# Where the squares of a norm run, in which order a list scheduler puts them, and when the next FFN may begin: one change to a two-layer trunk on eight cores

## The chip, the cores and the metric

The kernel runs on the eight cores of one Trainium2 chip. Each core holds 1280 of the 10240 tokens and does the whole computation for them. The metric is the device time of the slowest core in microseconds (us). Executions come in a fast and a slow state: in the slow one a die's cores show a lower granted clock.

Words used below: in this kernel TensorE (PE) does the matmuls, ScalarE (ACT) activations, VectorE (DVE) and GpSimd (POOL) elementwise work. FFN(l,s) is FFN s (0 or 1) of layer l. Its *first matmuls* make gate and up (22 pieces), its *second matmuls* bring the product back to 1024 channels. "Norm 6" is the RMSNorm in front of FFN(1,1), "norm 5" the one in front of layer 1's pooling, "norm 3" the one in front of FFN(0,1). *h* is a norm's shifted output (`sb_hbuf`), which the matmuls behind it read. A *bank* is one of the result buffers of TensorE (`ps`): the program writes it again only when ScalarE or VectorE has read it (in before, on core 6, TensorE stood 7.46 us until ScalarE had taken the first Silus, `sb_sg`, from theirs). A *gap* is time in which TensorE stands still.

## The reference, cut to what matters

```python
def run_trunk(x, ...):                       # x: (tokens, 1024)
    for l in range(2):
        mod = silu(cvec) @ ada_w[l] + ada_b[l]            # shifts, scales, gates
        x = x + 0.5 * g1 * swiglu(modulate(x, ...), ...)  # FFN(l,0)
        h = modulate(x, norm_g[l, 1], sh2, sc2)
        out = conv_attn_mixer(h, ...) if l == 0 else pool_mixer(h, ...)
        x = x + g2 * out
        x = x + 0.5 * g3 * swiglu(modulate(x, ...), ...)  # FFN(l,1)
    return rms_norm(x, final_g)
# modulate(x) = x * rsqrt(mean(x*x) + eps) * g * (1 + scale) + shift
# swiglu(h)   = (silu(h @ w1_gate) * (h @ w1_up)) @ w2, inner width 2816
# pool_mixer  = per channel group: (window mean - token) @ pool_w, window 2, 4, 8, 16
```

Seven norms, four FFNs, one attention and convolution mixer, one pooling mixer. The pooling of a token needs its neighbours up to 8 places away, so a tile's pooling needs the neighbouring tile's projected values.

## The kernel before

Activations stand transposed (channels on partitions, 8 chunks of 128) in three tiles of 512, 512 and 256 tokens. The program is written as small threads that yield operations; a list scheduler in Python commits one at a time and so fixes the instruction order on each engine before anything runs. The engines then go through their lists in order, waiting on semaphores: on core 6 of before ScalarE waits eight times, 0.55 to 0.64 us each, for VectorE's scalings between 1261 and 1274 us, and takes the first Silus of FFN(1,1), which stand behind in its list, only at 1276.41, though their matmuls run from 1254.42. What the scheduler thinks of time decides only the order:

```python
    def est(self, o):                        # class Sched
        t = self.free[o.eng]
        for d in self.deps_of(o):
            t = max(t, d.t_end)              # (cut)
        if o.tab is not None and o.tab != self.tab:
            t += 1280.0                      # ScalarE would have to load a table
        return t
    # run(): of all threads' next operations, on all engines, take the one with the
    # smallest (est, prio, seq).  Ln and Exp share a table, Silu has another.
```

The trace of before shows the tables on core 4: a load of 1.28 us ends just before tile 0's Ln at 43.37 us, Exp follows at 44.06 without one, and the next load, at 79.37, stands in front of the first Silus. The 18 loads take 1283 ns on average.

A norm: squares of 8 chunks by a plan, sums into `acc`, ones-matmuls over partitions on TensorE, Ln and Exp on ScalarE, then 8 scalings on VectorE (`sb_nt`) and 8 shifts on ScalarE (`sb_hbuf`, which the matmuls read).

```python
    def main(self):
        P8 = [(POOL, False)] * 6 + [(ACT, True)] * 2    # (engine of the square, summed by TensorE?)
        MX = [(ACT, False), (POOL, False), (ACT, False), (ACT, False),
              (POOL, False), (ACT, False), (ACT, True), (DVE, True)]
        ...
        yield from self.ffn(0, 1)
        self.prefetch(AF.Silu)
        S.spawn(self.mixer1(), 3)
        for t in range(3):
            S.spawn(self.norm(t, 5, 1, 1, P8), 0)
        yield from self.ffn(1, 0)
        for t in range(3):
            S.spawn(self.norm(t, 6, 1, 2, MX), 0)        # norm 6 enters the queues here
        yield self.wait("mix1done")                      # all 24 pooling residuals
        self.prefetch(AF.Silu)
        ...
        yield from self.ffn(1, 1)

    # mixer1, layer 1's pooling
        for t in range(3):
            yield self.wait(("h", t, 1, 1), 8)
            for i in range(4 * t, min(4 * t + 4, 10)):
                yield from ztile(i, t)                   # projection of tile t
            if t >= 1:
                ...
                yield from pout(t - 1)                   # pooling of the tile before
        yield from pout(2)
```

Weights stream through a ring of 512 KB slots (`sb_ring`); 72 of the slots are the modulation weights (`adaw`), strewn among the others.

The softmax here doesn't subtract the row's maximum and nothing guards it: scores larger than these inputs give would overflow.

Of the kernel before, what the change touches and what calls it, by code (L numbers as in the profile page):

```python
# [9 lines left out]
AF = mybir.ActivationFunctionType  # L10
# [35 lines left out]

class Op:
    __slots__ = ("eng", "fn", "reads", "writes", "cost", "is_dma", "nbytes", "key", "deps", "marked", "sig", "dval",
                 "t_end", "tab")

    def __init__(self, eng, fn, reads, writes, cost, is_dma=False, nbytes=0, key=None):
        self.eng, self.fn, self.reads, self.writes, self.cost = eng, fn, reads, writes, cost
        self.is_dma, self.nbytes, self.key = is_dma, nbytes, key
        self.deps = ()
        self.marked = False
        self.tab = None
        self.sig = 0
        self.dval = 0
        self.t_end = 0.0
# [17 lines left out]
class Sched:  # L77
# [56 lines left out]
    def est(self, o):  # L134
        t = self.free[o.eng]
        for d in self.deps_of(o):
            td = d.t_end
            if td > t:
                t = td
        if o.tab is not None and o.tab != self.tab:  # L140
            t += 1280.0
        return t

    def commit(self, o):
# [32 lines left out]
    def run(self):  # L177
        while self.threads:
            best, bk = None, None
            changed = False  # L180
            for t in sorted(self.threads, key=lambda t: (t.prio, t.seq)):
                while isinstance(t.head, Wait) and t.head.pred():
                    self.advance(t)
                    changed = True
                h = t.head
                if h is None or isinstance(h, Wait):
                    continue
                k = (self.est(h), t.prio, t.seq)
                if bk is None or k < bk:
                    best, bk = t, k  # L190
            if best is None:
                if changed:
                    continue
                raise RuntimeError("deadlock: %s" % [(t.prio, t.gen.__name__) for t in self.threads])
            self.commit(best.head)
            self.advance(best)
# [79 lines left out]
class Builder:  # L276
# [392 lines left out]
        d = self.dummy  # L669
        self.S.post([self.act(d[0:1, 0:1], d[0:1, 1:2], func, [self.b_dummy], [self.b_dummy])], 0)  # L670

    def rstd(self, t, ver, plan):

        c0, n, v = TILES[t]
        acc = None
        if not all(pe for e, pe in plan):
            acc = yield from self.take(self.accp)
        done, got = ("sumd", t, ver), {}

        def squares():  # L680
            first = True
            for d in range(8):
                e, pe = plan[d]
                yield self.wait(("x", t, d), ver)
                x, bxx = self.xres[:, d, c0:c0 + n], self.bx[t][d]
                if first and not pe:
                    first = False
                    yield self.square(e, acc[1][:, 0:n], x, bxx, acc[0])
                    self.sigl(done)
                    continue  # L690
                sq = yield from self.take(self.sqp)

                def one(e=e, pe=pe, x=x, bxx=bxx, sq=sq, d=d):
                    s = sq[1][:, 0:n]
                    yield self.square(e, s, x, bxx, sq[0])
                    if pe:
                        got[d] = sq
                    else:
                        a = acc[1][:, 0:n]
                        yield self.tt(a, a, s, ALU.add, [acc[0], sq[0]], [acc[0]], POOL if e == POOL else DVE)  # L700
                        self.sqp.give(sq)
                        self.sigl(done)
                self.S.spawn(one(), 1)
        self.S.spawn(squares(), 0)
        parts = ([] if acc is None else [None]) + [d for d in range(8) if plan[d][1]]
        nacc = sum(1 for e, pe in plan if not pe)
        k = None
        for q, d in enumerate(parts):
            if d is None:
                yield self.wait(done, nacc)  # L710
                src = acc
            else:
                yield Wait(lambda d=d: d in got)
                src = got[d]
            if k is None:
                k = yield from self.bank()
            yield self.mm([(self.psv(k, n), self.onesf[:], src[1][:, 0:n], q == 0, q == len(parts) - 1)],
                          [src[0], self.b_onesf], [self.psb[k]], f32=True)
            (self.accp if d is None else self.sqp).give(src)
        ps, pb = self.psv(k, n), self.psb[k]  # L720
        rs = yield from self.take(self.rsp)
        br, r = rs[0], rs[1][:, 0:n]
        yield self.act(r, ps, AF.Ln, [pb], [br], bias=EPS, scale=1.0 / D)
        self.unbank(k)
        yield self.act(r, r, AF.Exp, [br], [br], scale=-0.5)
        return rs

    def square(self, e, out, x, bx, bo):
# [1 line left out]
            return self.act(out, x, AF.Square, [bx], [bo])  # L730
        return self.tt(out, x, x, ALU.mult, [bx], [bo], e)

    def norm(self, t, ver, l, i, engs, hfree=None, sh=ACT):
        c0, n, v = TILES[t]
        rs = yield from self.rstd(t, ver, engs)
        br, r = rs[0], rs[1][:, 0:n]
        if hfree is not None:
            yield Wait(hfree)
        asc, msb = self.asc[l], self.modsb[l]
        for c in range(8):  # L740
            yield self.wait(("mod", l, i, c // 2), 2)
            bm = self.b_mod[l][3 * i][c // 2]
            nt = yield from self.take(self.ntp)
            bn, nv = nt[0], nt[1][:, 0:n]
            yield self.stt(nv, self.xres[:, c, c0:c0 + n], asc[:, i, c, v:v + 1], r, ALU.mult, ALU.mult,
                           [self.bx[t][c], br, self.b_asc[l][i][c // 2]], [bn])

            def fin(c=c, nt=nt, bn=bn, nv=nv, bm=bm):
                hv, b = self.hbuf[:, c, c0:c0 + n], msb[:, 24 * i + c, v:v + 1]
                if sh == ACT:  # L750
                    yield self.act(hv, nv, AF.Identity, [bn, bm], [self.bh[t][c]], bias=b, scale=1.0)
                else:
                    yield self.ts(hv, nv, b, None, ALU.add, None, [bn, bm], [self.bh[t][c]])
                self.ntp.give(nt)
                self.sigl(("h", t, l, i))
            self.S.spawn(fin(), 0)
        self.rsp.give(rs)


# [1 line left out]
    def ffn(self, l, s):  # L761
        S = self.S
# [4 lines left out]
        def room(t, j):  # L767
            lo = self.aoff(t) + j * TILES[t][1]
            if (l, s) == (0, 1):
                if not self.has("attndone"):  # L770
                    return False
                if not self.has("outmm", 3) and (t == 2 or (t == 0 and lo + 512 > self.q_lo)):
                    return False
            if (l, s) == (1, 1) and not self.has("mix1done"):
                return False
            if j not in NJT[t]:
                NJT[t][j] = self.abuf("a%d_%d" % (t, j), lo, lo + TILES[t][1])
# [111 lines left out]

    def main(self):  # L890
        S = self.S
        P8 = [(POOL, False)] * 6 + [(ACT, True)] * 2
        MX = [(ACT, False), (POOL, False), (ACT, False), (ACT, False), (POOL, False), (ACT, False), (ACT, True), (DVE, True)]
        IN = [(ACT, True), (DVE, True)] * 4
        for t in range(3):
            S.spawn(self.norm(t, 1, 0, 0, IN), 0)
        S.spawn(self.mixer0(), 3)
        for t in range(3):
            S.spawn(self.norm(t, 2, 0, 1, P8, sh=DVE if t == 2 else ACT), 0)
        yield from self.ffn(0, 0)  # L900
        for t in range(3):
            S.spawn(self.norm(t, 3, 0, 2, MX, hfree=lambda: self.has("convdone")), 0)
        for t in range(3):
            S.spawn(self.norm(t, 4, 1, 0, P8), 0)
        yield from self.ffn(0, 1)
        self.prefetch(AF.Silu)
        S.spawn(self.mixer1(), 3)
        for t in range(3):
            S.spawn(self.norm(t, 5, 1, 1, P8), 0)
        yield from self.ffn(1, 0)  # L910
        for t in range(3):
            S.spawn(self.norm(t, 6, 1, 2, MX), 0)
        yield self.wait("mix1done")
        self.prefetch(AF.Silu)
        for t in range(3):
            S.spawn(self.final(t, 7, P8), 0)
        yield from self.ffn(1, 1)


# [455 lines left out]
    def mixer1(self):  # L1375
        S = self.S
# [82 lines left out]
                    self.sigl("pout")  # L1459
                S.spawn(fin(), 1)  # L1460

        for t in range(3):
            yield self.wait(("h", t, 1, 1), 8)
            for i in range(4 * t, min(4 * t + 4, 10)):
                yield from ztile(i, t)
            if t >= 1:
                for i in range(0, 4 * t + (4 if t == 1 else 2)):
                    yield self.wait(("z", i), 2)
                yield from pout(t - 1)
        yield from pout(2)  # L1470
        self.wfree(("poolw",))
        yield self.wait("pout", 24)
        self.sigl("mix1done")

    def final(self, t, ver, engs):
        c0, n, v = TILES[t]
        rs = yield from self.rstd(t, ver, engs)
        br, r = rs[0], rs[1][:, 0:n]
# [153 lines left out]
```

## Time and profile before

| | before |
|---|---|
| time, fast runs | 1569.4 us median of 4 (1568.4 to 1570.6) |
| TensorE busy on the slowest core | 1464.3 of 1568.1 us |
| ScalarE, VectorE, GpSimd busy | 448.7, 500.1, 305.5 us |
| table loads on ScalarE | 18 |

The chain that ended last is 84% TensorE: whatever keeps TensorE from working costs time, and hardly anything else does. The prediction shows where it stands. The following view adds what the stretch of layer 1's pooling looks like in 20 us windows (busy us of each engine with the number of instructions, then granted clock, DMA share, GB/s; core 6):

```profile
core 6: us, PE busy (x) PEld busy (x) DVE busy (x) ACT busy (x) POOL busy (x), PEclk, DMA share, GB/s
1200.00:1220.00 20.00, 13.30 (x123) 11.28 (x121) 10.40 (x14) 3.42 (x7) 11.86 (x19) 0.92 0.35 53
1220.00:1240.00 20.00, 12.30 (x90) 8.41 (x90) 14.82 (x23) 11.01 (x20) 5.17 (x5) 0.74 1.03 161
1240.00:1260.00 20.00, 11.87 (x36) 5.37 (x37) 12.67 (x22) 9.96 (x16) 4.86 (x7) 0.66 0.56 103
1260.00:1280.00 20.00, 12.54 (x52) 5.26 (x51) 11.67 (x20) 13.61 (x25) 0.00 (x0) 0.87 0.00 0
```

For 80 us TensorE works 12 to 13 us in 20, at a clock down to 0.66, and no other compute engine is near full; the DMA queue is, in one of the four windows. That is a stage of waits, not of work.

I split the span at marks that are easy to find in TensorE's timeline of each core: the first of an FFN's second matmuls (they read `sb_areg` and `sb_ring`) and the first projection of the pooling. All stage times below are medians over eight cores.

### The profile page before, as it was taken

How to read it: one execution, taken by the hardware profiler on the slowest of the kernel's cores; microseconds unless marked ns; L12 is line 12 of the kernel's file. 1: busy time of each engine (PE TensorE's matmuls, PEld its weight loads, DVE VectorE, ACT ScalarE, POOL GpSimd, SP SyncE). 2: the span in 40 equal slices, each digit the busy share in tenths (PEclk: the TensorE clock that was granted, in tenths of full speed). 3: DMA queues.
4: the chain of work that ended last, by engine and by line, in shares of the span. 5: the costliest groups of instructions: out<-in, count | busy, mean ns of one | idle time of the engine just before them, and what ended most of it. 6: DMA issues, size and time to landing. Idle time of an engine off the chain costs nothing.

```text
span 1568.1 us, 26153 instructions; the slowest of 8 cores (1559.5 to 1568.1 us)
## 1 busy us (share of the span) xinstructions
PE 1464.3 (93%) x9662; PEld 807.7 (52%) x9662; DVE 500.1 (32%) x950; ACT 448.7 (29%) x734; POOL 305.5 (19%) x421
## 2 busy tenths in 40 slices
PE   2799999999999999999999989999999489999997
PEld 1355555457555554555544645555447245555445
DVE  0522222165833373222213322222135742222133
ACT  1521111034488954111102321111023441111001
POOL 3011102342321121100033411100333300000332
PEclk9999999999999999999999999999999699999999
DMA  9999832004579818954420199734022905330012
GB/s 170 210 172 169 132 63 46 7 11 80 87 120 172 139 25 128 140 76 61 69 39 1 27 167 173 132 54 68 14 43 34 155 1 95 56 66 14 1 54 82
DMA packets 41788, 131.48 MB, mean 84 GB/s; under 512 B 6336, under 2 KB 9152, under 8 KB 41664
## 3 DMA queue, kind: packets, MB, share of 16 engines
q0 software_dynamic: 34272, 120.42, 46.9%
q1 hardware_dynamic: 7392, 9.39, 2.0%
q8 instruction: 80, 1.31, 0.3%
q14 instruction: 44, 0.36, 0.1%
HBM read 240.50 MB, written 6.55 MB: 158 GB/s over the span
## 4 chain that ended last, share of the span: by engine, by line
PE 84%; DMA 7%; ACT 3%; DVE 3%; issue 2%; POOL 0%; DVEq 0%; SPq 0%; ACTq 0%; POOLq 0%
PE ps L294 84%; DMA sb_ring<-adaw 5%; DMA sb_xres<-xin 2%; DVE sb_nt L315 2%; ACT sb_hbuf L310 1%; ACT sb_sg L310 1%; ACT sb_rs L310 0%; PE ps L303 0%; DVE sb_xres L315 0%; ACT L310 0%; ACT sb_sq L310 0%; DVE sb_acc L320 0%; POOL sb_ring L345 0%; DVE sb_areg L320 0%; DVE sb_sg L320 0%
## 5 line engine op out<-in xcount | busy, mean ns | idle before, releaser
L294 PE MATMUL ps<-sb_hbuf,sb_ring 128*128 128x512 bf16 (+1 forms) x4512 | 843.0, 346 | 16.9 <-ACT sb_sg L310 13.8
L294 PEld LDWEIGHTS ps<-sb_hbuf,sb_ring 128*128 128x128 bf16 x4512 | 436.9, 98 | 385.1 <-issue 35.3
L294 PE MATMUL ps<-sb_areg,sb_ring 128*128 128x512 bf16 (+1 forms) x2304 | 425.9, 344 | 0.2
L320 DVE TENSOR_TENSOR sb_areg<-ps,sb_sg 128x512 bf16<-128x512 f32 (+1 forms) x264 | 157.6, 602 | 537.4 <-PE ps L294 508.6
L294 PEld LDWEIGHTS ps<-sb_areg,sb_ring 128*128 128x128 bf16 x2304 | 224.5, 98 | 196.5 <-issue 15.7
L310 ACT ACTIVATE sb_sg<-ps 128x512 f32<-128x512 f32 (+2 forms) x278 | 144.4, 526 | 617.9 <-PE ps L294 615.1
L315 DVE SCALAR_TENSOR_TENSOR sb_xres<-ps,sb_gsc,sb_xres 128x512 f32<-128x512 f32 (+1 forms) x152 | 96.6, 649 | 257.2 <-PE ps L294 257.0
L310 ACT ACTIVATE sb_sq<-sb_xres 128x512 f32<-128x512 f32 (+1 forms) x60 | 33.2, 557 | 349.2 <-DVE sb_xres L315 292.0
L315 DVE SCALAR_TENSOR_TENSOR sb_nt<-sb_xres,sb_asc,sb_rs 128x512 f32<-128x512 f32 (+1 forms) x144 | 101.7, 742 | 34.0 <-ACT sb_rs L310 23.9
L345 POOL DMA_DIRECT2D sb_ring<-w1t x88 | 47.8, 555 | 316.2 <-PE ps L294 313.4
L320 POOL TENSOR_TENSOR sb_sq<-sb_xres 128x512 f32<-128x512 f32 (+1 forms) x72 | 68.0, 946 | 180.4 <-DVE sb_xres L315 138.3
L310 ACT ACTIVATE sb_hbuf<-sb_nt,sb_modsb 128x512 bf16<-128x512 f32 (+1 forms) x136 | 86.2, 657 | 43.1 <-DVE sb_nt L315 42.6
L320 POOL TENSOR_TENSOR sb_acc<-sb_acc,sb_sq 128x512 f32<-128x512 f32 (+1 forms) x72 | 81.9, 1138 | 11.3 <-DVE sb_acc L320 1.8
L345 POOL DMA_DIRECT2D sb_ring<-w2t x44 | 23.4, 531 | 289.8 <-PE ps L294 283.8
L345 POOL DMA_DIRECT2D sb_ring<-adaw x72 | 39.1, 548 | 199.9 <-PE ps L294 195.2
L294 PE MATMUL ps<-sb_sq,sb_onesf 128*128 128x512 f32 (+1 forms) x120 | 56.7, 581 | 22.3 <-ACT sb_sq L310 21.4
L294 PE MATMUL ps<-sb_areg 128*128 128x65 bf16 (+3 forms) x592 | 64.6, 277 | 13.0 <-DVE sb_xres L315 8.0
L310 ACT ACTIVATE sb_sg<-ps,sb_amask 128x1024 bf16<-128x1024 f32 x65 | 71.3, 1114 | 10.9 <-PE ps L294 10.3
L294 PE MATMUL ps<-sb_scb,sb_ring 128*128 128x2 bf16 x1152 | 38.6, 163 | 27.9 <-DMA sb_ring<-adaw 26.7
L294 PEld LDWEIGHTS ps<-sb_scb,sb_ring 128*128 128x128 bf16 x1152 | 36.9, 96 | 41.6 <-issue 35.5
L294 PEld LDWEIGHTS ps<-sb_areg 128*128 128x128 bf16 (+1 forms) x592 | 29.7, 98 | 46.7 <-issue 43.9
L294 PE MATMUL ps<-sb_ring,sb_hbuf 128*128 128x256 bf16 x320 | 39.5, 280 | 10.6 <-ACT sb_hbuf L310 10.6
(71 smaller groups left out, 472.3 us busy)
## 6 DMA issues: line engine op xcount, KB each, us to landing
sb_ring<-w1t POOLq DMA_DIRECT2D x88, 512.0 KB, 12.6
sb_ring<-adaw POOLq DMA_DIRECT2D x72, 512.0 KB, 13.6
sb_ring<-w2t POOLq DMA_DIRECT2D x44, 512.0 KB, 5.6
sb_areg<-mp POOLq DMA_DIRECT2D x5, 512.0 KB, 7.1
sb_xres<-xin SPq DMA_DIRECT2D x2, 1024.0 KB, 24.4
sb_xres<-xin POOLq DMA_DIRECT2D x2, 1024.0 KB, 43.4
sb_ring<-wcx POOLq DMA_DIRECT2D x4, 512.0 KB, 11.6
sb_ring<-wo POOLq DMA_DIRECT2D x4, 512.0 KB, 9.6
```

Source lines behind the costliest of these rows:

```text
L294: ins = e.matmul(m[0], lhsT=m[1], rhs=m[2], start=m[3], stop=m[4], **({"skip_group_check": True} if len(m) > 5 else {}))
L310: o = Op(ACT, lambda e: e.activation(out=out, in_=in_, func=func, **kw), reads, writes, cost)
L315: return Op(DVE, lambda e: e.scalar_tensor_tensor(out=out, in0=in0, scalar=scalar, in1=in1, op0=op0, op1=op1), reads, writes, 150.0 + 1.04 ...
L320: return Op(eng, lambda e: e.tensor_tensor(out=out, in0=in0, in1=in1, op=op), reads, writes, c)
L345: return Op(q, lambda e: e.dma_start(out=out, in_=in_), reads, writes, 600.0 if q == POOL else 450.0, True, nbytes, key)
```

## The change

Its intent is to take the squares from GpSimd, to let the scheduler put each tile's norm where it is wanted, and to let FFN(1,1) begin under layer 1's pooling. The core of the diff:

```diff
     def est(self, o):
-        if o.tab is not None and o.tab != self.tab:
-            t += 1280.0
         return t
@@ run
-                k = (self.est(h), t.prio, t.seq)
+                k = (self.est(h), t.prio if h.p is None else h.p, t.seq)
@@ rstd
+        yield self.wait(("x", t, 0), ver)          # before it takes a sum buffer
...
-        yield self.act(r, r, AF.Exp, [br], [br], scale=-0.5)
+        o = self.act(r, r, AF.Exp, [br], [br], scale=-0.5)
+        o.p = -9
+        yield o
@@ ffn: room
-            if (l, s) == (1, 1) and not self.has("mix1done"):
+            if (l, s) == (1, 1) and not self.has("poutmm", 2 if t == 0 else 3):
@@ main
+        A8 = [(ACT, False)] * 6 + [(ACT, True)] * 2
+        def norms(ver, l, i, plan, sh=(ACT,) * 3, hfree=None):
+            for t in range(3):
+                p = -1 + 0.1 * t if i == 1 else (0, 1.5, 2)[t]
+                S.spawn(self.norm(t, ver, l, i, plan, prio=p, sh=sh[t], hfree=hfree), p)
+        norms(1, 0, 0, IN)
+        norms(2, 0, 1, P8, sh=(ACT, ACT, DVE))
+        norms(3, 0, 2, A8, hfree=lambda: self.has("convdone"))
+        norms(4, 1, 0, A8)
+        norms(5, 1, 1, A8)
+        norms(6, 1, 2, A8)                         # all spawned before the first FFN
...
         yield from self.ffn(1, 0)
-        for t in range(3):
-            S.spawn(self.norm(t, 6, 1, 2, MX), 0)
-        yield self.wait("mix1done")
-        self.prefetch(AF.Silu)
...
         yield from self.ffn(1, 1)
@@ mixer1
+        yield from zs(0)                           # zs: projection of a tile
+        yield from zs(1)
+        yield from po(0)                           # po: pooling, then signal "poutmm"
+        yield from po(1)
+        self.prefetch(AF.Silu)
+        yield from zs(2)
+        yield from po(2)
```

I group it in three parts: the **plans** (squares on ScalarE, sums on VectorE), the **pooling** (new order in mixer1, and the new condition in `room`, which says when a piece of an FFN may start; I call it the gate), and the **order** (table switch no longer charged, all norms spawned at the start, priorities by tile, Exp first).

More of the change, by code (lines that the diff above doesn't have):

```diff
@@ L48 @@
     __slots__ = ("eng", "fn", "reads", "writes", "cost", "is_dma", "nbytes", "key", "deps", "marked", "sig", "dval",
-                 "t_end", "tab")
+                 "t_end", "tab", "p")
     def __init__(self, eng, fn, reads, writes, cost, is_dma=False, nbytes=0, key=None):
@@ L56, in __init__ @@
         self.tab = None
+        self.p = None
         self.sig = 0
@@ L670, in prefetch, with rstd @@
         self.S.post([self.act(d[0:1, 0:1], d[0:1, 1:2], func, [self.b_dummy], [self.b_dummy])], 0)
-    def rstd(self, t, ver, plan):
+    def rstd(self, t, ver, plan, prio=0):
         c0, n, v = TILES[t]
         acc = None
+        yield self.wait(("x", t, 0), ver)
         if not all(pe for e, pe in plan):
@@ L702, in one @@
                         self.sigl(done)
-                self.S.spawn(one(), 1)
-        self.S.spawn(squares(), 0)
+                self.S.spawn(one(), prio)
+        self.S.spawn(squares(), prio)
         parts = ([] if acc is None else [None]) + [d for d in range(8) if plan[d][1]]
@@ L731, in square, with norm @@
         return self.tt(out, x, x, ALU.mult, [bx], [bo], e)
-    def norm(self, t, ver, l, i, engs, hfree=None, sh=ACT):
+    def norm(self, t, ver, l, i, engs, prio=0, hfree=None, sh=ACT):
         c0, n, v = TILES[t]
-        rs = yield from self.rstd(t, ver, engs)
+        rs = yield from self.rstd(t, ver, engs, prio)
         br, r = rs[0], rs[1][:, 0:n]
@@ L755, in fin @@
                 self.sigl(("h", t, l, i))
-            self.S.spawn(fin(), 0)
+            self.S.spawn(fin(), prio)
         self.rsp.give(rs)
@@ L891, in main @@
         S = self.S
+        A8 = [(ACT, False)] * 6 + [(ACT, True)] * 2
         P8 = [(POOL, False)] * 6 + [(ACT, True)] * 2
-        MX = [(ACT, False), (POOL, False), (ACT, False), (ACT, False), (POOL, False), (ACT, False), (ACT, True), (DVE, True)]
         IN = [(ACT, True), (DVE, True)] * 4
+        def norms(ver, l, i, plan, sh=(ACT,) * 3, hfree=None):
[8 more added lines that the diff above has]
+        norms(6, 1, 2, A8)
         for t in range(3):
-            S.spawn(self.norm(t, 1, 0, 0, IN), 0)
+            S.spawn(self.final(t, 7, A8), 0)
         S.spawn(self.mixer0(), 3)
-        for t in range(3):
-            S.spawn(self.norm(t, 2, 0, 1, P8, sh=DVE if t == 2 else ACT), 0)
         yield from self.ffn(0, 0)
-        for t in range(3):
-            S.spawn(self.norm(t, 3, 0, 2, MX, hfree=lambda: self.has("convdone")), 0)
-        for t in range(3):
-            S.spawn(self.norm(t, 4, 1, 0, P8), 0)
         yield from self.ffn(0, 1)
@@ L907, in main @@
         S.spawn(self.mixer1(), 3)
-        for t in range(3):
-            S.spawn(self.norm(t, 5, 1, 1, P8), 0)
         yield from self.ffn(1, 0)
-        for t in range(3):
-            S.spawn(self.norm(t, 6, 1, 2, MX), 0)
-        yield self.wait("mix1done")
-        self.prefetch(AF.Silu)
-        for t in range(3):
-            S.spawn(self.final(t, 7, P8), 0)
         yield from self.ffn(1, 1)
@@ L1460, in pout, with zs @@
                 S.spawn(fin(), 1)
-        for t in range(3):
+        def zs(t):
             yield self.wait(("h", t, 1, 1), 8)
@@ L1465, in mixer1, with po @@
                 yield from ztile(i, t)
-            if t >= 1:
-                for i in range(0, 4 * t + (4 if t == 1 else 2)):
-                    yield self.wait(("z", i), 2)
-                yield from pout(t - 1)
-        yield from pout(2)
+        def po(t):
+            for i in range(0, (5, 8, 10)[t]):
+                yield self.wait(("z", i), 2)
+            yield from pout(t)
+            self.sigl("poutmm")
+        yield from zs(0)
[5 more added lines that the diff above has]
+        yield from po(2)
         self.wfree(("poolw",))
-        yield self.wait("pout", 24)
-        self.sigl("mix1done")
     def final(self, t, ver, engs):
+        yield self.wait(("x", t, 0), ver)
         c0, n, v = TILES[t]
```

## The prediction

> **What bounds the kernel now.** I read the page first: what is the busiest engine, and where is it not busy.
>
> ```profile
> PE 1464.3 (93%) x9662; PEld 807.7 (52%) x9662; DVE 500.1 (32%) x950; ACT 448.7 (29%) x734; POOL 305.5 (19%) x421
> ...
> PE   2799999999999999999999989999999489999997
> ...
> PEclk9999999999999999999999999999999699999999
> ```
>
> TensorE is the bound almost everywhere, and its work does not change: both programs have 1442 groups of matmuls. What can be won is its idle time, 1568.1 - 1464.3 = 104 us, and what it loses to a lower clock after a gap. Both show in slice 32 (1215 to 1255 us): busy 4 tenths, clock 6. I then cut the span into stretches of 20 us. The idle time is 41 us up to 100 us, 8 between 420 and 560, 4 between 580 and 640, 2 at 790, 7 between 880 and 920, 30 between 1180 and 1280, the rest (12) mostly at the end. The timeline of TensorE shows what ends each gap in the 30 us, which is layer 1's pooling:
>
> ```profile
> 1215.18 0.67 PE L294 MATMUL ps<-sb_sq,sb_onesf 128*128 128x256 f32 x2 [2.55 <-ACT sb_sq L310]
> 1224.04 1.01 PE L294 MATMUL ps<-sb_ring,sb_hbuf 128*128 128x256 bf16 x4 [8.18 <-ACT sb_hbuf L310]
> ...
> 1244.36 0.58 PE L294 MATMUL ps<-sb_areg 128*128 128x256 bf16 x2 [6.59 <-DVE sb_xres L315]
> ...
> 1260.03 9.66 PE L294 MATMUL ps<-sb_hbuf,sb_ring 128*128 128x512 bf16 x44
> 1277.15 5.14 PE L294 MATMUL ps<-sb_hbuf,sb_ring 128*128 128x512 bf16 x13 [7.46 <-ACT sb_sg L310]
> ```
>
> The reader sees a serial chain: tile 2's norm (8.18), the residual of pooling (6.59), then banks that only come free when ScalarE, busy with two tiles' norms, gets to its first Silu (7.46). Why tile 2's norm is so late shows on VectorE and GpSimd in the same microseconds:
>
> ```profile
> 1216.94 5.44 DVE L315 SCALAR_TENSOR_TENSOR sb_nt<-sb_xres,sb_asc,sb_rs 128x256 f32<-128x256 f32 x3 [2.47 <-ACT sb_rs L310]
> 1222.69 0.48 DVE L315 SCALAR_TENSOR_TENSOR sb_nt<-sb_xres,sb_asc,sb_rs 128x256 f32<-128x256 f32 x1 [0.31 <-ACT sb_hbuf L310]
> ...
> 1216.95 2.13 POOL L320 TENSOR_TENSOR sb_sq<-sb_xres 128x512 f32<-128x512 f32 x2
> 1218.95 2.75 POOL L320 TENSOR_TENSOR sb_acc<-sb_acc,sb_sq 128x512 f32<-128x512 f32 x2
> ```
>
> Three scalings of 0.48 us each took 5.44 us, exactly as long as GpSimd was at tile 0's squares and sums. At the start of the kernel the same kind of bank wait stands:
>
> ```profile
> 72.33 1.89 PE L294 MATMUL ps<-sb_hbuf,sb_ring 128*128 128x512 bf16 x8 [0.73 <-ACT sb_rs L310]
> 76.45 0.55 PE L294 MATMUL ps<-sb_scb,sb_ring 128*128 128x2 bf16 x16 [2.23 <-DMA sb_ring<-adaw]
> 80.56 8.51 PE L294 MATMUL ps<-sb_hbuf,sb_ring 128*128 128x512 bf16 x32 [3.56 <-ACT sb_sg L310]
> ```
>
> [...] 13 matmuls in 5.14 us (0.40 each) after the 7.46 us gap, 44 in 9.66 us (0.22) before it. [...] The trace has 18 loads with a mean of 1283 ns; the load at 41.23 us ends at 42.51 and the next activation starts at 42.52, [...] and I charge 1.28 us.
>
> **The change, part by part.** (1) For five of the seven norms the six squares and five sums that GpSimd did for each tile (P8), or four engines in a mix (MX), become squares on ScalarE and sums on VectorE; the last two squares still go to TensorE as ones-matmuls, so its part is unchanged. In the instruction streams GpSimd goes from 417 to 294 entries (minus 123), VectorE from 950 to 1001, ScalarE from 716 to 788. By the rows of groups, a 512-wide square is 1075 ns on GpSimd and 629 on ScalarE, a sum 1299 on GpSimd and 684 on VectorE. Cost: 72 x at most 0.63 = 45 us more on ScalarE (449 of 1568 busy) and 51 x at most 0.68 = 35 us on VectorE (500 busy). None of it lies on TensorE's path in the FFN stages, where the squares of a tile trickle in behind second matmuls of 4.7 us each.
>
> (2) The scheduler no longer charges the table switch when it chooses what is next. From the order of ScalarE's program I count switches between Silu and Ln/Exp: 18 before (as many as the trace has loads), 26 after. So 8 x 1.28 = 10 us more on ScalarE, five of them at the start. In exchange the first Silus come before the norms of tiles 1 and 2 and free banks. On TensorE 56 matmuls of tile 0 (12.3 us at 0.22) now stand where before it waited. The gaps from 62 to 93 us are 0.64 + 0.32 + 0.73 + 2.23 + 3.56 + 0.95 = 8.4 us; the 32 matmuls that took 8.51 us at a lowered clock should take 7.0. The weights are there in time: 6.3 MB land between 45.9 us (first FFN matmul) and 76.2 us (end of the wait for adaw), so by that pace (an estimate) slot 2 is in at 58, slot 3 at 66, slot 4 at 69, slot 5 at 71, each just before TensorE wants it (63, 67, 70, 74). ScalarE, with its loads, is through the first Silus at 63.4, 64.0, 67.8, 71.6 us, before their banks are wanted again. Tile 1's norm slips by 5 us, to about 80, while TensorE has tile 0's work until 85. Gain 8.4 + 1.5, less a microsecond: **9 us**.
>
> (3) Pooling by tile. I stepped the new program order from 1180.1 us (first pooling projection), with durations of before. Up to 1197.3 all is as before. Pooling of tile 0 is 8 x 0.53 us (56 matmuls in 4.26), and tile 1's follows without the wait for tile 2; the remaining 99 FFN matmuls of tile 2 (0.11 each, 11 us) are strewn among it as filler. With three ones-sums (2.75) TensorE comes to the next FFN's first matmul at 1219.3. The chain beside it: VectorE evacuates and adds without a break from 1198 to 1213 (16 x 0.66 to 0.75, 6 x 0.6), always just ahead of the bank that is wanted; last square of tile 0 at 1207.2, sums to 1211.1, Ln 1211.9. A Silu prefetch falls between Ln and Exp (two loads, 2.8 us), Exp ends at 1215.4, first scaled piece 1216.3, first piece of h at 1217.2: 2 us ahead of TensorE. Further pieces come about every 0.9 us; four matmuls for each take 0.88. After that tile 0 alone has 22 x 3.5 us of work, which covers the norms of tiles 1 and 2 and pooling of tile 2. Weights: the second matmul's ring slots come free some 6 us later (1218 instead of 1211), four first-matmul slots are loaded already, and one slot lands every 3.1 us (512 KB at 170 GB/s), used every 3.5. So the eight gaps, 30.2 us, go. At the lowered clock 1.0 + 1.6 us (the ones-sums at 1249 to 1254 took 2.04 + 3.45 instead of 1.02 + 1.88), 2.2 us (after 1277) and small ones at 1224 and 1244 come back, 5 together. I leave 3 us for gaps that I did not see: **32 us**.
>
> (4) The other two FFN starts wait for adaw slots (1.72 and 3.90 us at 900 and 907; 1.63 and smaller at 599 to 637), and that is the pace of loads. At 588 the output projection now ends before the FFN starts, so slots free 3.5 us earlier: 2 us. At 907 one piece moves in front of the wait: 1 us. **3 us**. Attention (the same 100 exponentials, the same matmuls, order a little different) and the last norm (8 us from the last matmul to the end, same chain): **0**.
>
> Sum 9 + 32 + 3 = 44; 1569.7 - 44 = 1526.
>
> **Rivals.** (a) Loads of tables and squares make ScalarE the bound: for it, 26 loads and the prefetch inside the norm; against, ScalarE is at most 10 of 20 us busy in those stages. If all 10 us of loads came out on the path: 1536. (b) VectorE becomes the bound in pooling, since it evacuates, adds and scales alone: my stepping leaves under 1 us of slack for some banks. 20% slower there is 3 us, with the norm chain 5: 1531. (c) The start is paced by loads (DMA share 1.0 up to 160 us), so the early gain is lost later: for it, the full queue; against, TensorE waits only once for a load between 60 and 240 us. Then 1535. (d) Squares in front of exponentials: ScalarE is 19 of 20 us busy from 520 to 540, and an in-order square that waits for a residual can hold them: 4 us, 1530. (e) Nothing moves, because filler only moves a wait to where the filler stood: against it, tile 0's new work needs nothing that tile 2 has to finish. Above 1545 by that.
>
> **Range.** (a) to (d) can come in part together, and none gives a slowdown of the whole. 1513 to 1544; faster by over 2% (below 1538) 0.85, within 2% 0.14, slower 0.01.
>
> **What would show it.** TensorE's gaps between 1170 and 1240 under 5 us and the clock near 1 there; no gap over 1 us between 62 and 95; 26 table loads; GpSimd near 180 us busy (123 entries at about 1.05 us fewer); scalings of h at 0.5 to 0.8 us everywhere outside attention. I am wrong if waits on ScalarE's hbuf or Silu over 2 us stand in the pooling, or if the FFN starts wait longer for slots.

## The result, and the profile after

| | before | after |
|---|---|---|
| time, fast runs, median | 1569.4 us (4 runs) | 1519.1 us (4 runs, 1516.4 to 1520.1) |
| ratio | | 0.9677 (95%: 0.9660 to 0.9693) |

The ratio is the mean time of one kernel's fast runs over that of the other's of the same rounds, so it is not quite the ratio of the medians. The gain is 3.2%, 50 us where 44 were predicted. The page of the profile after (core 0; busy times, TensorE and its clock in 40 slices):

```profile
PE 1442.7 (95%) x9516; PEld 806.5 (53%) x9662; DVE 513.7 (34%) x1001; ACT 494.0 (33%) x814; POOL 177.3 (12%) x298
...
PE   2899999999988999999999989999999999999997
...
PEclk8999999999999999999999999999999999999999
```

Slice 32 is no longer a hole. TensorE's smaller busy time is in part a gap in the records (9516 of 9662 matmuls, so a slice without waits shows 19.9 of 20), in part the clock (mean 0.986 on this core, 0.974 on core 6 of before). The same windows as before, on the same core 6:

```profile
1200.00:1220.00 20.00, 19.89 (x119) 12.59 (x120) 14.98 (x29) 17.62 (x33) 5.84 (x11) 1.00 0.57 90
1220.00:1240.00 20.00, 19.89 (x107) 10.60 (x107) 15.01 (x28) 15.40 (x27) 0.54 (x1) 1.00 1.04 170
```

and TensorE's timeline on core 0 (start, duration, instruction, count, and in brackets the idle time before it and what ended it). The start of the kernel:

```profile
64.25 12.25 PE L293 MATMUL ps<-sb_hbuf,sb_ring 128*128 128x512 bf16 x54
...
95.04 5.21 PE L293 MATMUL ps<-sb_hbuf,sb_ring 128*128 128x256 bf16 x31 [1.74 <-ACT sb_sg L309]
```

and the pooling, where no line from 1169 to 1260 us carries a bracket:

```profile
1169.32 2.35 PE L293 MATMUL ps<-sb_ring,sb_hbuf 128*128 128x256 bf16 x20
...
1207.48 1.67 PE L293 MATMUL ps<-sb_hbuf,sb_ring 128*128 128x512 bf16 x7
```

FFN(1,1) begins 38.2 us after the pooling's first projection; before it was 74.3 (1180.1 to 1254.4 on core 6). By stage:

| stage | before | after | change | predicted |
|---|---|---|---|---|
| start to FFN(0,0)'s second matmuls | 268.0 | 261.0 | -7.0 | -9 |
| from there to FFN(0,1)'s second matmuls (mixer of layer 0 in it) | 521.8 | 519.7 | -2.1 | -2 |
| from there to FFN(1,0)'s second matmuls | 305.8 | 303.5 | -2.3 | -1 |
| FFN(1,0)'s second matmuls to the pooling | 80.3 | 80.3 | 0 | 0 |
| pooling to FFN(1,1)'s second matmuls | 275.5 | 237.0 | -38.5 | -32 |
| last matmuls | 103.3 | 103.3 | 0 | 0 |

The sum is -49.9. So the total came out near, and by stage too. Whether it came from the *parts of the change* that I named is another question, and there the experiments surprised me.

### The profile page after: what moved, and what is told of

The parts are those of the page before. It is cut to its first block, busy times and chain, and to the rows that moved or that the text cites. A ratio compares the mean times of both kernels' runs of the same rounds, so it can differ in the third digit from the quotient of the medians.

```text
span 1518.6 us, 25939 instructions; the slowest of 8 cores (1504.6 to 1518.6 us)
## 1 busy us (share of the span) xinstructions
PE 1442.7 (95%) x9516; PEld 806.5 (53%) x9662; DVE 513.7 (34%) x1001; ACT 494.0 (33%) x814; POOL 177.3 (12%) x298
## 4 chain that ended last, share of the span: by engine, by line
PE 88%; DMA 7%; issue 2%; ACT 2%; DVE 1%; SPq 0%; DVEq 0%; POOL 0%; ACTq 0%; POOLq 0%
PE ps L293 87%; DMA sb_ring<-adaw 4%; DMA sb_xres<-xin 2%; DVE sb_nt L314 1%; ACT sb_sg L309 0%; ACT sb_areg L309 0%; PE ps L302 0%; DVE sb_areg L319 0%; ACT sb_hbuf L309 0%; ACT sb_rs L309 0%; DVE sb_sg L319 0%; ACT L309 0%; DMA yo<-sb_nt 0%; ACT sb_sq L309 0%; SPq L344 0%
## 5 line engine op out<-in xcount | busy, mean ns | idle before, releaser
L293 PE MATMUL ps<-sb_hbuf,sb_ring 128*128 128x512 bf16 (+1 forms) x4405 | 832.4, 345 | 14.6 <-ACT sb_sg L309 4.9
L293 PE MATMUL ps<-sb_areg,sb_ring 128*128 128x512 bf16 (+1 forms) x2265 | 420.5, 343 | 2.4 <-ACT sb_sg L309 0.2
L309 ACT ACTIVATE sb_sq<-sb_xres 128x512 f32<-128x512 f32 (+1 forms) x123 | 68.1, 556 | 299.1 <-DVE sb_xres L314 240.8
L314 DVE SCALAR_TENSOR_TENSOR sb_nt<-sb_xres,sb_asc,sb_rs 128x512 f32<-128x512 f32 (+1 forms) x144 | 90.7, 664 | 28.8 <-ACT sb_rs L309 21.1
L293 PE MATMUL ps<-sb_areg 128*128 128x65 bf16 (+3 forms) x584 | 61.4, 271 | 3.7 <-ACT sb_st L309 2.0
L319 DVE TENSOR_TENSOR sb_acc<-sb_acc,sb_sq 128x512 f32<-128x512 f32 (+1 forms) x75 | 45.1, 601 | 34.5 <-ACT sb_sq L309 33.2
L293 PEld LDWEIGHTS ps<-sb_sq,sb_onesf 128*128 128x128 f32 x120 | 23.0, 203 | 34.3 <-issue 30.3
L319 DVE TENSOR_TENSOR sb_modsb<-ps,sb_adab 128x4 f32<-128x4 f32 x72 | 11.5, 160 | 83.2 <-PE ps L293 83.1
```

The costliest lines, as they stand in the source:

```text
L293: ins = e.matmul(m[0], lhsT=m[1], rhs=m[2], start=m[3], stop=m[4], **({"skip_group_check": True} if len(m) > 5 else {}))
L309: o = Op(ACT, lambda e: e.activation(out=out, in_=in_, func=func, **kw), reads, writes, cost)
L314: return Op(DVE, lambda e: e.scalar_tensor_tensor(out=out, in0=in0, scalar=scalar, in1=in1, op0=op0, op1=op1), reads, writes, 150.0 + 1.04 ...
L319: return Op(eng, lambda e: e.tensor_tensor(out=out, in0=in0, in1=in1, op=op), reads, writes, c)
```

## The experiments

Medians are over fast runs; "x slower than after" compares with 1519.1 us. After itself was not run again, so that a difference of 2 or 3 us to after is near the noise. All twelve kernels gave correct results.

**One part put in, one part taken out.** Theory A (parts add up by stage, the pooling's order matters) against rival B (the squares on GpSimd held the stage).

*e1*, before with the new plans alone:

```diff
+        A8 = [(ACT, False)] * 6 + [(ACT, True)] * 2
-            S.spawn(self.norm(t, 4, 1, 0, P8), 0)
+            S.spawn(self.norm(t, 4, 1, 0, A8), 0)
(cut: the same for norms 3, 5 and 6 and the final one)
```

> Kernel before with only the new plans of the squares (ScalarE squares, VectorE sums, last two chunks by TensorE) for norms 3 to 6 and the final one; order and pooling as before. Theory A (the parts add up by stage, and the pooling's order is what mattered): only the tails of norms get shorter, at the starts of FFN(0,1) and FFN(1,0) and after the pooling, together 5 to 12 us: 1558 to 1565. Rival B (the squares on GpSimd, through the longer scalings beside them, were what held the pooling stage): at least 25 us: below 1545, and the gaps of TensorE after the pooling's start shrink from 30 us to under 12.

Measured 1551.1 us, ratio 0.9887 (0.9868 to 0.9907): 17 us, between the two. TensorE's gaps after the pooling's start are 14.0 us on core 0 instead of 30.2; the one in front of tile 2's h is 2.97 instead of 8.18, the one in front of the first Silus 2.81 instead of 7.45.

*e2*, before with the new pooling alone (mixer1 and `room` as in after, no wait for "mix1done" in main):

> Kernel before with only the new pooling of layer 1 (tile by tile, FFN(1,1) allowed once two tiles' pooling matmuls are out); squares still on GpSimd, order as before. Theory A: about 28 to 38 us faster, 1531 to 1541, TensorE's gaps after the pooling's start under 8 us. Rival B: 5 to 15 us, 1554 to 1564, since norm 6's squares on GpSimd take over as the wait. The mean scaling of 128x512 in that stretch stays above 0.75 us by both.

Measured 1555.7 us, ratio 0.9916 (0.9897 to 0.9936): 13 us, in rival B's range. Its TensorE timeline (core 0) still has

```profile
1222.66 1.01 PE L294 MATMUL ps<-sb_ring,sb_hbuf 128*128 128x256 bf16 x4 [8.10 <-ACT sb_hbuf L310]
```

the same wait for tile 2's h that before has (8.18).

*e3*, after with the old plans put back:

> Kernel after with the old plans of the squares put back (GpSimd squares and sums in norms 3 to 6 and the final one), order and pooling as after. Theory A: 4 to 12 us slower than after, 1523 to 1531. Rival B: 25 us or more slower, above 1544.

Measured 1522.2 us, ratio 0.9705 (0.9679 to 0.9732): 3 us slower than after, less than even theory A asked, and hardly above the noise (1519.5 to 1524.7, after 1516.4 to 1520.1). This is the run that strikes at my reading of the profile before. The scalings are slow again, as the groups of VectorE show (count, busy us, mean ns; core 4 of after, then core 4 of e3):

```profile
L314 DVE SCALAR_TENSOR_TENSOR sb_nt<-sb_xres,sb_asc,sb_rs 128x512 f32<-128x512 f32 x96 | 69.2, 755 | 21.3 <-ACT sb_rs L309 17.2 <-ACT sb_hbuf L309 3.7
```

```profile
L314 DVE SCALAR_TENSOR_TENSOR sb_nt<-sb_xres,sb_asc,sb_rs 128x512 f32<-128x512 f32 x96 | 74.9, 814 | 21.1 <-ACT sb_rs L309 15.2 <-ACT sb_hbuf L309 5.6 <-DVE sb_nt L314 0.2
```

In the pooling, four of them took 4.37 us, 1.09 each, while GpSimd was at its squares and sums (core 4):

```profile
1198.39 4.37 DVE L314 SCALAR_TENSOR_TENSOR sb_nt<-sb_xres,sb_asc,sb_rs 128x512 f32<-128x512 f32 x4
```

But hardly any TensorE wait hangs on them now: the wait for tile 2's h is 0.34 us.

*e4*, after with the old pooling put back:

> Kernel after with the old pooling put back (next tile's projection before a tile's pooling, FFN(1,1) only after all pooling residuals), plans and order as after. Theory A: the stage's gain is lost, 25 to 38 us slower than after, 1544 to 1557. Rival B: 5 to 15 us slower, 1524 to 1534, since the faster squares alone close most of the gaps.

Measured 1536.7 us, ratio 0.9796 (0.9774 to 0.9817): 18 us slower, between the two. The pooling stage is 252.1 us, its largest gap 7.13 us, again before tile 2's projection, which the old order wants before it pools tile 1. GpSimd has no squares here, so it is not what holds tile 2's h: on core 4 VectorE does all eight of tile 0's scalings for norm 6, from 1196.87 to 1204.79 us, before all but one of tile 2's for norm 5.

Neither theory stands. The plans are worth 17 us in the old order and 3 in the new one; the pooling 13 and 18. The third part, the order, had to be tested. Theory C: what matters is when norm 6 enters the queues.

*e5*, before with plans and pooling, without the order:

> Kernel before with the new plans and the new pooling, without the new order (norms spawned where they were, table switch charged, no priorities by tile). Theory C, formed on the first four runs: what holds the pooling stage is that the norms before FFN(1,1) are put into the queues only after FFN(1,0) is written out; so plans and pooling together stay near the sum of their single gains (17 + 13 us): 1535 to 1545, and TensorE still waits over 2 us for tile 2's h and for the first Silu. Rival A: plans and pooling are what matters and the order gives only the start's 9 us: 1524 to 1531, no gap over 2 us after the pooling's start.

Measured 1558.8 us, ratio 0.9926 (0.9902 to 0.9950). Two parts that gain 17 and 13 alone gain 12 together. Both theories missed. TensorE and ScalarE of core 4 tell why:

```profile
1232.12 3.35 PE L294 MATMUL ps<-sb_hbuf,sb_ring 128*128 128x512 bf16 x8 [4.55 <-ACT sb_hbuf L310]
...
1266.38 53.92 PE L294 MATMUL ps<-sb_hbuf,sb_ring 128*128 128x512 bf16 x298 [6.91 <-ACT sb_sg L310]
```

```profile
1240.01 0.58 ACT L310 ACTIVATE sb_rs<-ps 128x512 f32<-128x512 f32 x1
1241.10 0.61 ACT L310 ACTIVATE sb_rs<-sb_rs 128x512 f32<-128x512 f32 x1
1257.06 0.38 ACT L310 ACTIVATE sb_rs<-ps 128x256 f32<-128x256 f32 x1 [1.27 <-PE ps L294]
1257.53 0.42 ACT L310 ACTIVATE sb_rs<-sb_rs 128x256 f32<-128x256 f32 x1
1263.26 1.28 ACT L310 ACT_TABLE_LOAD   x1
1264.56 2.08 ACT L310 ACTIVATE sb_sg<-ps 128x512 f32<-128x512 f32 x4
```

FFN(1,1)'s first matmul runs at 1232.12, its first Silu only at 1264.56, 32 us later: ScalarE's list has the Ln and Exp (`sb_rs`) of all three tiles in front (tile 0's Ln is at 1227.66), then one table load, then the four Silus in a row. The matmuls' banks are full meanwhile, and TensorE waits 6.91 us. FFN(1,1)'s first matmul had itself waited 4.55 us for tile 0's h. FFN(1,1) begins earlier than in e1 (50.9 against 59.3 us after the pooling's start) and takes longer (212.5 against 199.8). The 7.46 us in front of `sb_sg` in before is the same thing.

*e6*, the order alone (after with old plans and old pooling):

> Kernel after with both the old plans and the old pooling: only the new order is left. Theory C (plans matter little once the order is by tile, as they did with the new pooling, 3 us): 1538 to 1544. Rival (the plans' 17 us is a gain of its own kind that only the new pooling hides): 1549 to 1556. Start and end of attention as in the kernel after, within 2 us, by both.

Measured 1538.9 us, ratio 0.9798 (0.9781 to 0.9815). Theory C's range. The order alone is 32 us, the largest of the three.

| fast median, us | old order | new order |
|---|---|---|
| neither plans nor pooling | 1569.4 | 1538.9 |
| plans | 1551.1 | 1536.7 |
| pooling | 1555.7 | 1522.2 |
| both | 1558.8 | 1519.1 |

*e7*, after with the table charge put back:

```diff
+        if o.tab is not None and o.tab != self.tab:
+            t += 1280.0
         return t
```

> Kernel after, but the scheduler again charges 1280 ns for a switch of table when it chooses what is next. My prediction's part 2 says that the start's gain hangs on this: FFN(0,0)'s second matmuls start some 7 us later than in the kernel after, near 268, and the total is 5 to 10 us slower, 1524 to 1529, with 18 to 22 table loads. Rival (the start's gain comes of priorities by tile and of the early spawn): within 2 us of the kernel after, start unchanged.

Measured 1550.8 us, ratio 0.9873 (0.9850 to 0.9897): 32 us slower than after. My own figure, 5 to 10, was a quarter of it. The profile fell into a slow run, so I read die 1 (cores 4 to 7, clock 0.98). The start is 267.8 us, 6.8 more than after, as predicted, with 18 table loads; TensorE waits 4.88 us for the first Silus there. But the stretch to FFN(0,1)'s second matmuls takes 533.8 instead of 519.7, and the pooling stage 243.6 instead of 237.0. In front of FFN(0,1) two tiles' Ln and Exp are put off until ScalarE has nothing else (core 4):

```profile
578.62 1.28 ACT L311 ACT_TABLE_LOAD   x1
579.92 0.87 ACT L311 ACTIVATE sb_rs<-ps 128x512 f32<-128x512 f32 x2
580.67 0.94 ACT L311 ACTIVATE sb_rs<-sb_rs 128x512 f32<-128x512 f32 x2
```

In after the first of them stands at 556.49. (On this core after's last attention exponential is also 7 us earlier, so about 16 of the 23 us are the norm's own delay.)

*e8*, after with norm 6 and the final norms spawned after FFN(1,0), as in before:

```diff
-        norms(6, 1, 2, A8)          (at the start of main)
...
         yield from self.ffn(1, 0)
+        norms(6, 1, 2, A8)
```

> Kernel after, but the norms before FFN(1,1) and the final ones are spawned after FFN(1,0) has been written out, as in before. All engines' programs are those of the kernel after up to the pooling stage. Theory C: 12 to 22 us slower than after, 1531 to 1541, all of it between the pooling's start and FFN(1,1)'s second matmuls, with a gap over 2 us at FFN(1,1)'s first matmul or first Silu. Rival (pooling tile by tile is enough, and scheduling only fills): at most 4 us slower, below 1524.

Measured 1532.7 us, ratio 0.9759 (0.9742 to 0.9776): 14 us slower, theory C's range. The pooling stage is 248.3 us, FFN(1,1) begins 52.1 us after its start. On core 4:

```profile
1209.94 0.67 PE L293 MATMUL ps<-sb_sq,sb_onesf 128*128 128x256 f32 x2 [2.03 <-ACT sb_sq L309]
1214.10 2.04 PE L293 MATMUL ps<-sb_acc,sb_onesf 128*128 128x512 f32 x2 [3.49 <-DVE sb_acc L319]
...
1221.43 2.69 PE L293 MATMUL ps<-sb_ring,sb_hbuf 128*128 128x256 bf16 x12 [2.10 <-ACT sb_hbuf L309]
```

The waits stand in front of the norms' sums and tile 2's h; I had expected them at FFN(1,1) itself. Tile 0's norm comes so late that its FFN isn't there as filler.

Theory D: the table charge is the order's main piece. *e9*, before with that one piece of the diff alone (the two lines of `est` removed):

> Kernel before with one thing alone: the scheduler no longer charges 1280 ns for a switch of table when it chooses. Theory D (formed on the run with the charge put back, 31 us slower than after): this line carries most of the order's gain, 20 to 32 us: 1538 to 1550, with FFN(0,0)'s second matmuls near 261 and the stretch from attention's end to FFN(0,1)'s second matmuls some 8 us shorter than in before. Rival (the line only pays together with priorities by tile and the early spawn): 5 to 12 us, 1557 to 1565, all at the start.

Measured 1547.5 us, ratio 0.9857 (0.9838 to 0.9875): 22 us from two lines. The profile is of a slow run; on die 1 the start is 259.6 us, the stretch to FFN(0,1)'s second matmuls 514.6 instead of 521.8, the pooling stage 266.2 instead of 275.5. The waits for tile 2's h (8.25) and the pooling's residual (6.59) are all there, but the 7.45 us in front of the first Silus is gone, because ScalarE now switches (core 4):

```profile
1234.41 1.28 ACT L308 ACT_TABLE_LOAD   x1 [5.80 <-PE ps L292]
1235.70 0.60 ACT L308 ACTIVATE sb_rs<-ps 128x512 f32<-128x512 f32 x1
...
1241.63 1.28 ACT L308 ACT_TABLE_LOAD   x1
1242.92 0.60 ACT L308 ACTIVATE sb_sg<-ps 128x512 f32<-128x512 f32 x1
```

It loads 26 tables instead of 18 (33.4 us of ScalarE's time instead of 23.1), and the kernel is 22 us faster.

*e10*, after with FFN(1,1) held until the pooling matmuls of all three tiles are out:

```diff
-            if (l, s) == (1, 1) and not self.has("poutmm", 2 if t == 0 else 3):
+            if (l, s) == (1, 1) and not self.has("poutmm", 3):
```

> Kernel after, but FFN(1,1) may begin only when the pooling matmuls of all three tiles are out (for tile 0 too); everything else as in after, and the programs are the same up to the pooling stage. Theory C (what counts is that TensorE has tile 0's FFN while tile 2's norm and pooling run): 8 to 18 us slower than after, 1527 to 1537, with a wait of TensorE for tile 2's h of 4 us or more. Rival (FFN matmuls of tile 2 before it fill the time as well): within 3 us of after.

Measured 1536.3 us, ratio 0.9799 (0.9779 to 0.9819): 17 us slower, 15 of it in the pooling stage (252.1 against 237.0). The gaps of core 4 there sum to 10.4 us, the longest 3.29 in front of a sum and 2.90 for tile 2's h, so the wait for h is smaller than I expected; the rest of the 15 us, 4.6, I put down to a lowered clock. That is my estimate, from one reading: after the gap of 1.94 us two ones-matmuls took 2.05 us instead of 1.02. In e4, where the order in mixer1 is the old one as well, the stage takes the same 252.1 us. So with the old gate, pooling tile by tile is worth nothing in this stage; its use is that it lets the gate open while tile 2 is still to be projected.

*e11*, after with all norms at priority 0:

```diff
-                p = -1 + 0.1 * t if i == 1 else (0, 1.5, 2)[t]
+                p = 0
```

> Kernel after, but all norms have priority 0 instead of one by tile; early spawn, table charge off, plans and pooling as in after. If the order by tile is a real part of the gain: 5 to 15 us slower, 1524 to 1534, with later first h of tile 0 at the FFN starts. If the scheduler's time estimates order the tiles anyway: within 3 us of after, 1516 to 1522.

Measured 1526.5 us, ratio 0.9728 (0.9707 to 0.9749): 7 us slower, so the priorities are a real part. The pooling stage is as in after (237.1); the largest loss in any stage median is 2.4 us, in the stretch to FFN(0,1)'s second matmuls. On the two slowest cores, 2 and 5, that stretch takes 527.3 and 528.5 us, where no core of after takes more than 522.5. TensorE's waits for Silu in it sum to 5.7 to 5.9 us on every core, in after to 0.6 to 1.8: some 4.5 of the 7 us, and the same wait again. The rest I did not settle. "Exp first" and the wait before a norm takes its sum buffer were never tested alone.

*e12*, an attempt at a faster kernel: after, with slower loads assumed by the scheduler from layer 0's mixer on:

```diff
     def mixer0(self):
         yield self.wait(("w2t", 0, 0, 0))
+        S.DMA_RATE = 220.0
```

The reason was that between the first and the last of attention's value matmuls the kernel after takes 134 us, before 128 (medians over the cores), and that TensorE waits there for `adaw` slots: summed over the timeline from 400 to 560 us, 1.0 to 7.0 us per core, where before has 1.5 to 3.1.

> Kernel after with one line more, an attempt at a faster one: from the first mixer on the scheduler assumes that weights land at 220 GB/s instead of 315 (the traces show about 170 with the queue full), so it places the small adaw matmuls some 3 to 8 us later in attention. If attention's loss (133 us against 128 in before) is TensorE waiting in order for adaw slots that land later than assumed: 3 to 6 us faster than after, 1513 to 1516, and the cores' spans closer together. If the loss is ScalarE's exponentials: no change or slower, 1519 to 1525.

Measured 1518.0 us, ratio 0.9671 (0.9656 to 0.9687): the same as after. The waits for `adaw` fell to 0.6 us at most, but those for ScalarE rose from 3.8 to 5.2 us per core to 5.4 to 6.9, and the stretch to FFN(0,1)'s second matmuls stayed (519.6 against 519.7). The cores moved together (spans 1509.1 to 1517.4, after 1504.6 to 1518.6). The first and last value matmuls turn out to be a bad mark, since what is interleaved moves them; the stretch as a whole is not longer in after than in before. No experiment gave a version that beats after.

## Why the prediction was right or wrong, point by point

**What bounds the kernel.** Right: TensorE's idle time and its clock (0.974 on the slowest core before, 0.986 after) were all that there was to win.

**Part 2, the start (9 us).** Right in mechanism, 7.0 measured. ScalarE's list at the start, before and after, both on core 4:

```profile
72.55 0.38 ACT L310 ACTIVATE sb_rs<-ps 128x256 f32<-128x256 f32 x1 [0.84 <-PE ps L294]
73.44 0.40 ACT L310 ACTIVATE sb_rs<-sb_rs 128x256 f32<-128x256 f32 x1
79.37 1.28 ACT L310 ACT_TABLE_LOAD   x1
80.66 2.08 ACT L310 ACTIVATE sb_sg<-ps 128x512 f32<-128x512 f32 x4
```

```profile
61.92 1.28 ACT L309 ACT_TABLE_LOAD   x1 [1.08 <-PE ps L293]
63.22 1.08 ACT L309 ACTIVATE sb_sg<-ps 128x512 f32<-128x512 f32 x2
64.32 1.28 ACT L309 ACT_TABLE_LOAD   x1
65.61 0.60 ACT L309 ACTIVATE sb_rs<-ps 128x512 f32<-128x512 f32 x1
66.23 1.28 ACT L309 ACT_TABLE_LOAD   x1
```

The first Silus come at 63.22 instead of 80.66, at the price of a load before nearly every activation. The step that failed is what I let this part do: "five of them at the start. In exchange the first Silus come before the norms of tiles 1 and 2 and free banks" was worked out for the start alone. The charge acts wherever a norm and an FFN meet on ScalarE. Taking it away is worth 22 us in the old kernel (e9), putting it back costs 32 in the new one (e7). I counted the eight extra loads as a cost for the whole kernel and their use for one stage of it. In the stage of the pooling I read the 7.46 us in front of Silu as the last link of a serial chain that goes when the chain is cut; e5 cuts the chain and has 6.91 us there.

**Part 1, the plans.** I booked them as a cost beside TensorE's path, and that is so: ScalarE's 45.3 us more, loads included, left no gap in the pooling. But "Why tile 2's norm is so late shows on VectorE and GpSimd" was read as if the slow scalings were the cause to be removed. ("Exactly as long" was also misread: the three took 5.44 us, of which the first took 3.64, and GpSimd was at its squares and sums for 4.76.) In the old order the plans do shorten the wait for tile 2's h, from 8.18 to 2.97 us (e1); since they make squares and sums faster too (128x512: 1075 ns on GpSimd in before, 629 on ScalarE; 1299 on GpSimd, 689 on VectorE in after), e1 does not show that the slow scalings alone were the cause. In the new order they are not: with GpSimd back the scalings are slow again and 3 us are lost (e3), and without GpSimd but with the old pooling the wait is still 7.13 us (e4). A delay is worth what waits for it.

**Part 3, the pooling (32 us).** Right in mechanism; FFN(1,1) came 38.2 us after the pooling's start where my stepping said 39.2, the Silu prefetch did fall between Ln and Exp, and the eight gaps went. The sum was mis-sized in two terms. "At the lowered clock ... 5 together": on core 6 the stage was 275.8 us, of which 30.2 were gaps and so 245.6 work; after it is 236.9 us with no gap on record, so the same work took 8.7 us longer before. The clock accounts for nearly all of it: in three stretches of 34.1 us together (1216.75 to 1230.38, 1240.64 to 1254.28 and 1274.77 to 1281.58) it stood at 0.50, and TensorE was busy 15.5 us of them, by my estimate (15.5 x 0.50) work of 7.8 us at a clock of 1.00. In the stage of after it stood at 1.00. Slow matmuls followed short gaps as well: on core 4 of e5, after gaps of 1.89 and 2.05 us with 0.67 us of work between, two ones-matmuls took 2.05 us, where two of the same kind took 1.02 at 1235.30. "I leave 3 us for gaps that I did not see": there were none. 30.2 + 8.7 = 38.9 on this core, where I had 30.2 + 5 - 3 = 32. What I did not see is how many things the stage needs at once: undo the early spawn (14 us lost, e8), the gate (17, e10), the gate and the pooling order together (18, e4) or put back the charge (7 of its 32 in this stage, e7), and much of it comes back.

**Part 4 (3 us, attention and tail 0).** 4.4 measured for the two stretches. The step "that is the pace of loads" failed for FFN(0,1): its waits for `adaw` (1.93, 1.02, 0.71, 0.94 us on core 4 before) are gone there in after, with the same loads (on core 0 one of 1.80 is left), while those in attention grew to as much as 7.0 us on one core. Attention itself came out even in the stretch that I can trust, and the tail is the same 103.3 us.

**Rivals.** (a) did not come: 26 loads as counted, and no gap in the pooling, though ScalarE is 17.62 of 20 us busy in the window 1200 to 1220. (My "at most 10 of 20 us busy in those stages" was misread: before has 13.61 in the window 1260 to 1280.) At the start of FFN(1,0) TensorE does wait 2.69 us for a Silu on core 6, where the waits in before were 1.72 and 3.90 us for `adaw`. (b) did not: VectorE is 15 of 20 busy there, and no gap. (c) came in part, as waits for slots in attention, which e12 shows not to be what counts. (d) did not show: TensorE's waits for ScalarE in attention are 4.2 to 4.6 us per core before, 3.8 to 5.2 after. (e) did not.

**What would show it.** Gaps from 1170 to 1240: none, clock 1.00. Table loads: 26. GpSimd 177.3 us busy (180 said). Scalings of h 755 and 481 ns on average. One sign failed: there is a gap of 1.74 us before 95 us, where tile 2's first matmuls wait for a Silu.

## What to carry to other kernels

In a program whose order is fixed by a list scheduler, a cost in the scheduler's estimate is a decision about order: charging a 1.28 us table load made it save eight loads and cost 22 to 32 us, because results that free buffers waited behind work that only happened to share the table. Count what a switch holds up, not only what it takes. And test parts of a change in both directions: here one part was worth 17 us or 3, and two parts with gains of 17 and 13 gave 12 together, since both moved the wait on to what neither removes, the place of the norms and Silus in ScalarE's list (in e5 4.55 us for tile 0's h and 6.91 for the first Silus).
